# Reciprocal square roots of norms on VectorE: nine two-tensor steps against seven one-tensor steps

## The chip, the cores and the metric

One Trainium2 chip, one of its cores. The time is that of one execution of the whole program on the device, in microseconds (us); a smaller one is better. The program has five engines that matter here: TensorE (PE, with its weight loads PEld), VectorE (DVE), ScalarE (ACT), GpSimd (POOL) and SyncE (SP), which issues the DMAs. Each works through its own queue in order.

## What is computed

Two blocks of a network on one sequence of 1024 tokens with 1024 features, in float32. The first block has a layer A (a gated linear recurrence beside latent attention) and an SSD layer (a chunked state-space scan); the second has a gated feed-forward, a mixing layer (dilated attention beside a diagonal state-space model) and a second feed-forward. What matters here are the norms, one reciprocal root for each token (and, in the SSD layer, for each group of 512 features):

```python
def _rmsnorm(x, g, eps=1e-6):
    y = xf * lax.rsqrt(jnp.mean(xf * xf, axis=-1, keepdims=True) + eps)
def _layernorm(x, g, b, eps=1e-5):
    y = xc * lax.rsqrt(var + eps) * g + b
...
    yg = yg * lax.rsqrt(jnp.mean(yg * yg, axis=-1, keepdims=True) + 1e-6)
...
        x = x + 0.5 * rms_norm(swiglu(h, ...), ffn_post_g)
        h = rms_norm(x, mix_pre_g)
```

## The kernel before

Products run on TensorE in float32r, with every factor split into a high and a low part (`split`, L138 to L141: ScalarE copies the high part, VectorE or GpSimd subtracts). Tokens lie on the 128 partitions in the parts that concern us, in 8 tiles of 128 tokens, so a norm needs one number for each partition: a column of 128x1.

`rsqrt_col` (L264) makes the reciprocal root of such a column on VectorE, with no table of ScalarE. It forms a = v * scale + eps (L270), a first guess from the bits of a taken as an integer (L271), turns a into -a/2 (L272), and makes three Newton rounds of a product c = (y * a) * y (L275) and a step y = (c + 1.5) * y (L280); a factor `mul` other than 1 costs one more instruction (L282). At L275 the operand `a` stands in the place of a scalar read from a column, while `y` is read as two tensors; at L280 `c` and `y` are two tensors and 1.5 is an immediate. Each instruction needs the result of the one before.

Its callers, all with one column but the first:

- `low` in layer A (L485): two calls with 8 columns at once, before the latent projections, at about 82 and 115 us. Here the product is made with two tensor_tensors (L277, L278).
- `layernorm` (L659, called in `layer_a_out` and in `SsdOut.rest`): 16 calls, tile `rl`. VectorE's L667 and ScalarE's L668 follow, then the gain at L669 (VectorE or GpSimd) and the bias at L670 (GpSimd).
- `norm` in the SSD layer (L963): 32 calls, tile `rs`. ScalarE's square (L967) is in front, ScalarE's scaling (L969) behind; `flip` (L971) then transposes on TensorE and evicts on ScalarE (L977).
- `pre_norm` (L1113): 24 calls, tile `rp`, in `SsdOut.rest`, at the end of the first feed-forward and in `mix_out`. ScalarE squares (L1108), VectorE adds the halves (L1110), ScalarE scales (L1118), and TensorE transposes the result.
- `post_norm` (L1121): 24 calls, tile `ro`: 16 at the ends of the two feed-forwards, with `mul` 0.5, and 8 in `mix_out`, with `mul` 1. VectorE sums the tile from PSUM before it (L1428, L1781), scales behind it (L1126, two tensors from SBUF), and GpSimd adds the residual (L1127; VectorE for the last two tiles).

After `SsdOut.rest` and `mix_out` the operands of the next feed-forward are built from the normed tiles (`Ops.build`, L1153, with sums of quarters at L1177 to L1183, some splits of it on GpSimd), and its weights are combined on GpSimd (L1220 to L1223) and split on VectorE.

In the SSD layer, GpSimd makes four products a chunk (L923, L931 to L933) beside VectorE's clamp of 1024 columns (L924).

The order of instructions on each engine isn't the order of the code alone. The program is traced under a context that plans it from modelled durations of the instructions:

```python
    with tile.TileContext(nc, schedule_with_timeline_sim=True) as tc:   # L1947
```

`issue_after`, `deferred` and `behind` add bounds to that plan by hand, for the products and for some loads.

Of the kernel before, what the change touches and what calls it, by code (L numbers as in the profile page):

```python
# [13 lines left out]
I32 = mybir.dt.int32  # L14
AF = mybir.ActivationFunctionType
ALU = mybir.AluOpType
# [247 lines left out]
def rsqrt_col(K, out, v, n, scale, eps, mul=1.0, tag="rs"):  # L264


    V = K.nc.vector
    t = K.small(3 * n, f"{tag}{n}", bufs=2 if n == 1 else 1)
    a, y, c = (t[:, j * n:(j + 1) * n] for j in range(3))
    V.tensor_scalar(a, v, scale, eps, ALU.mult, ALU.add)  # L270
    V.tensor_scalar(y.bitcast(I32), a.bitcast(I32), -0.5, 1597463007.0, ALU.mult, ALU.add)  # L271
    V.tensor_scalar(a, a, -0.5, None, ALU.mult)  # L272
    for step in range(3):
        if n == 1:
            V.scalar_tensor_tensor(c, y, a, y, ALU.mult, ALU.mult)  # L275
        else:
            V.tensor_tensor(c, y, y, ALU.mult)  # L277
            V.tensor_tensor(c, c, a, ALU.mult)  # L278
        last = step == 2
        V.scalar_tensor_tensor(out if last and mul == 1.0 else y, c, 1.5, y, ALU.add, ALU.mult)  # L280
    if mul != 1.0:
        V.tensor_scalar(out, y, mul, None, ALU.mult)  # L282


def sin_tables(K, pos, cos, sin, ang, n):
# [118 lines left out]
def layer_a(K, I, XT, get):  # L404
# [62 lines left out]
    def low(c0, nt, name, scale):  # L467
        raws = []
        rq = K.Q2()
        ssq = K.B()  # L470
        for m in range(nt):
            a = K.A()
            proj_fm(K, a, wload(K, w_in[:, :, c0 + m * P:c0 + (m + 1) * P], NK, P), get)
            raw, sq = rq[:, m, :], K.S()
            nc.scalar.activation(raw, a, AF.Copy)
            nc.scalar.activation(sq, a, AF.Square)
            for i in range(NT):
                nc.tensor.matmul(ssq[:, m * 8 + i:m * 8 + i + 1], sq[:, i * P:(i + 1) * P], K.ones, start=True, stop=True)
            raws.append(raw)
        r = K.small(8, "rst" + name, bufs=1)  # L480
        v = K.small(8, "rsv" + name, bufs=1)
        nc.vector.tensor_copy(v, ssq[:, 0:8])
        for m in range(1, nt):
            nc.vector.tensor_tensor(v, v, ssq[:, m * 8:m * 8 + 8], ALU.add)
        rsqrt_col(K, r, v, 8, scale, 1e-6)  # L485
        outs = [K.Q2(F32R) for _ in range(nt)]
        for h in range(2):
            b = K.B()
            for q in range(4):
                nc.tensor.matmul(b[:, q * P:(q + 1) * P], r[:, 4 * h + q:4 * h + q + 1].to_broadcast([P, P]), K.ident, start=True, stop=True)  # L490
            for m in range(nt):
                rw = raws[m][:, h * 512:h * 512 + 512]
                nc.vector.scalar_tensor_tensor(rw, rw, col(K, name, m), b, ALU.mult, ALU.mult)
                split(K, outs[m][:, 0, h * 512:h * 512 + 512], outs[m][:, 1, h * 512:h * 512 + 512], rw)
        return outs
# [163 lines left out]
def layernorm(K, z, g, b, pool=False):  # L659

    nc = K.nc
    t = K.small(16, "lnt", bufs=3)
    for h in range(2):
        nc.vector.bn_stats(t[:, 6 * h:6 * h + 6], z[:, 512 * h:512 * h + 512])
    nc.vector.bn_aggr(t[:, 12:14], t[:, 0:12].rearrange("p (a b) -> p a b", a=2))
    rsqrt_col(K, t[:, 14:15], t[:, 13:14], 1, 1.0, 1e-5, tag="rl")
    nc.vector.scalar_tensor_tensor(t[:, 15:16], t[:, 12:13], -1.0, t[:, 14:15], ALU.mult, ALU.mult)  # L667
    nc.scalar.activation(z, z, AF.Identity, bias=t[:, 15:16], scale=t[:, 14:15])  # L668
    (nc.gpsimd if pool else nc.vector).tensor_tensor(z, z, g, ALU.mult)  # L669
    nc.gpsimd.tensor_tensor(z, z, b, ALU.add)  # L670
# [111 lines left out]
def ssd_layer(K, I, get, yd, out):  # L782
# [180 lines left out]
    def norm(n):  # L963
        _, _, xdt, sz, y, _ = held[n]
        nc.vector.tensor_tensor(y, y, sz, ALU.mult)
        t = K.small(2, "yss", bufs=3)
        nc.scalar.activation(xdt, y, AF.Square, accum_out=t[:, 0:1])  # L967
        rsqrt_col(K, t[:, 1:2], t[:, 0:1], 1, 1.0 / 512, 1e-6)
        nc.scalar.activation(y, y, AF.Copy, scale=t[:, 1:2])  # L969
# [981 lines left out]
```

## Time and profile before

| | us |
|---|---|
| median of 3 runs | 3380.14 |
| lowest, highest | 3374.5, 3385.84 |
| the profiled execution's own time | 3382.45 |
| its span in the trace | 3380.6 |

The span runs from the first to the last instruction in the trace; the execution's own time has what lies around it too. In the rows below, L275 is line 275 of the kernel, `ro<-ro` a tile written and read (numbers of buffers left out), `128x1` partitions by columns. A wait in square brackets is idle time of the engine in front of an instruction, with what ended it. A duration of VectorE runs from the start of an instruction to its end, and so includes the time that it stands in the engine without progress.

### The profile page before, as it was taken

What the parts mean: (1) busy time and instruction counts of PE and PEld (TensorE: products, weight loads), DVE (VectorE), ACT (ScalarE), POOL (GpSimd) and SP (SyncE); (2) the same over time, 40 slices, a digit from 0 to 9 for tenths busy, and PEclk for the clock granted to TensorE, in tenths of its full rate; (3) what the DMA queues carried; (4) which work ended last, traced back from release to release, by engine and by line L of the source; (5) the groups of instructions that cost most, each with busy time, mean ns of one, the idle gap of its engine ahead of it and who ended that gap; (6) DMA issues with size and microseconds to landing.
All of it is one profiled execution on the core that took longest, in us unless ns stands there. A gap on an engine that the chain in (4) does not pass through costs nothing. (4 is left out here: it accounts for less than half of the span.)

```text
span 3380.6 us, 42313 instructions
## 1 busy us (share of the span) xinstructions
PE 3094.7 (92%) x15560; PEld 2578.1 (76%) x15560; DVE 2295.6 (68%) x3819; ACT 1628.1 (48%) x2947; POOL 774.4 (23%) x487
## 2 busy tenths in 40 slices
PE   8999898999999888878999989899899699999997
PEld 6877877878787776667778877678787588888776
DVE  6537777275848455888785689835676955555998
ACT  5526534354545422465555434542475655554442
POOL 0000011122322211432233345100000423232543
PEclk9999999999999899989999999999999899999999
DMA  3157342244334544323332520435454422224322
GB/s 126 61 191 229 99 144 83 73 83 109 90 103 87 161 147 135 109 83 125 108 125 87 206 86 27 156 125 212 137 154 137 152 75 76 87 81 139 117 81 112
DMA packets 344959, 398.98 MB, mean 118 GB/s; under 512 B 20656, under 2 KB 270640, under 8 KB 344752
## 3 DMA queue, kind: packets, MB, share of 16 engines
q1 hardware_dynamic: 344752, 396.28, 37.8%
q8 instruction: 123, 2.02, 0.2%
q14 instruction: 84, 0.69, 0.1%
HBM read 279.29 MB, written 116.92 MB: 117 GB/s over the span
## 5 line engine op out<-in xcount | busy, mean ns | idle before, releaser
L141 DVE TENSOR_TENSOR wlo<-wst,whi 128x1024 fp32r<-128x1024 f32 (+1 forms) x190 | 230.4, 1216 | 353.6 <-ACT whi L140 344.8
L185 PE MATMUL pa<-x,whi 128*128 128x512 f32 x1568 | 433.9, 398 | 20.6 <-ACT l L343 14.9
L185 PEld LDWEIGHTS pa<-x,whi 128*128 128x128 f32 x1568 | 294.7, 190 | 85.8 <-ACT l L343 15.8
L140 ACT ACTIVATE whi<-wst 128x1024 fp32r<-128x1024 f32 (+1 forms) x190 | 180.1, 949 | 361.2 <-PE pa L185 94.9
L147 ACT ACTIVATE wst<-wst,pk 128x128 f32<-128x128 f32 (+1 forms) x816 | 251.5, 391 | 185.2 <-DMA wst<-in_ffn_w_in_dram 114.8
L185 PE MATMUL pa<-x,wlo 128*128 128x512 f32 x784 | 245.2, 394 | 3.8 <-DVE wlo L141 3.8
L1257 PE MATMUL pb<-x,whi 128*128 128x512 f32 (+1 forms) x736 | 224.5, 381 | 0.0
L1257 PE MATMUL pa<-x,whi 128*128 128x512 f32 (+1 forms) x736 | 220.7, 382 | 0.6 <-DVE p L1271 0.4
L1336 PE MATMUL pa<-wlo,whi 128*128 128x512 f32 x768 | 186.7, 400 | 15.4 <-DVE wlo L141 13.3
L1336 PE MATMUL pb<-wlo,whi 128*128 128x512 f32 x744 | 181.5, 401 | 14.4 <-DVE wlo L141 14.4
L1336 PEld LDWEIGHTS pa<-wlo,whi 128*128 128x128 f32 x768 | 147.6, 193 | 52.0 <-DVE wlo L141 18.2
L1220 POOL TENSOR_TENSOR s<-wst 128x512 f32<-128x512 f32 x44 | 56.9, 1294 | 568.0 <-ACT wst L147 532.3
L1336 PEld LDWEIGHTS pb<-wlo,whi 128*128 128x128 f32 x744 | 142.9, 193 | 48.9 <-DVE wlo L141 19.1
L185 PEld LDWEIGHTS pa<-x,wlo 128*128 128x128 f32 x784 | 148.2, 190 | 38.3 <-DVE wlo L141 6.4
L923 POOL TENSOR_TENSOR s<-s,p 128x1024 f32<-128x1024 f32 x32 | 62.0, 1939 | 499.2 <-DMA s<-d 425.2
L880 PE MATMUL pa<-whi,x 128*128 128x256 f32 x512 | 149.3, 292 | 11.6 <-ACT l L889 8.6
L1257 PEld LDWEIGHTS pa<-x,whi 128*128 128x128 f32 x736 | 136.3, 189 | 28.0 <-ACT p L1260 1.4
L1257 PEld LDWEIGHTS pb<-x,whi 128*128 128x128 f32 x736 | 136.3, 189 | 26.4 <-issue 0.4
L881 PE MATMUL pa<-wlo,x 128*128 128x256 f32 x512 | 145.8, 285 | 0.0
L882 PE MATMUL pa<-whi,x 128*128 128x256 f32 x512 | 145.7, 285 | 0.0
L140 ACT ACTIVATE whi<-s 128x1024 fp32r<-128x1024 f32 x88 | 93.0, 1057 | 107.2 <-POOL s L1221 56.8
L684 PE MATMUL pa<-whi,s 128*128 128x512 f32 x448 | 132.1, 401 | 9.6 <-ACT s L140 4.6
(581 smaller groups left out, 8048.0 us busy)
## 6 DMA issues: line engine op xcount, KB each, us to landing
wst<-in_ffn_w_in_dram SPq DMA_DIRECT2D x88, 512.0 KB, 3.8
d<-l SPq DMA_DIRECT2D x83, 512.0 KB, 3.4
d<-p SPq DMA_DIRECT2D x82, 512.0 KB, 3.5
x<-d SPq DMA_DIRECT2D x128, 256.0 KB, 5.4
p<-d SPq DMA_DIRECT2D x46, 512.0 KB, 4.9
wst<-in_s_w_in_dram SPq DMA_DIRECT2D x40, 512.0 KB, 4.1
s<-d SPq DMA_DIRECT2D x32, 512.0 KB, 9.5
l<-d SPq DMA_DIRECT2D x24, 512.0 KB, 5.8
```

The costliest lines, as they stand in the source:

```text
L140: K.nc.scalar.activation(hi, src, AF.Copy)
L141: (eng or K.nc.vector).tensor_tensor(lo, src, hi.bitcast(F32), ALU.subtract)
L147: K.nc.scalar.activation(st[:, k, :], st[:, k, :], AF.Copy, scale=col(K, gain, k0 + k))
L185: K.nc.tensor.matmul(ps[:, h:h + 512], w, x[:, h:h + 512], start=k == 0 and m == 0, stop=k == n - 1 and m == 2)
L684: K.nc.tensor.matmul(ps[:, h:h + 512], l, r[:, h:h + 512], start=k == 0 and m == 0, stop=k == n - 1 and m == 2)
L880: nc.tensor.matmul(o, xh, wh, start=k == 0, stop=False)
L881: nc.tensor.matmul(o, xh, wl, start=False, stop=False)
L882: nc.tensor.matmul(o, xl, wh, start=False, stop=k == NK - 1)
L923: nc.gpsimd.tensor_tensor(mv, mv, per_head(csT, P), ALU.subtract)
L1220: G(s1, a21, a22, ALU.add)
L1257: nc.tensor.matmul(p, l[:, k, :], r[:, k, :], start=k + m == 0, stop=k == 3 and m == 2)
L1336: nc.tensor.matmul(bank[j], th[:, a + o:a + o + P], tw[:, b:b + 512], start=c + m == 0, stop=c == n - 1 and m == 2)
```

## The change

`rsqrt_col` alone changes. The value and its factor go into one column h = -(v * scale + eps) / (2 mul^2), by one instruction; the guess is taken from the bits of h, with the constant adjusted for its sign, its half and a scaling k. Then come a Newton round (a square c = (y * y) * h and a step y = (c + 1.5 k^(2/3)) * y) and a round of third order (a square and two steps), with constants that spread the error. The factor `mul` costs no instruction of its own. For one column each of these is a `tensor_scalar`: one tensor and two scalars, of which the squares read both from columns, and the steps one from a column and one from the instruction. For 8 columns the steps are scalar_tensor_tensors with an immediate, and the squares two tensor_tensors. A call makes 7 instructions in place of 9 (or of 10 with a factor), and with 8 columns 9 in place of 12.

```diff
--- before.py
+++ after.py
@@ -264,22 +264,33 @@
 def rsqrt_col(K, out, v, n, scale, eps, mul=1.0, tag="rs"):
 
 
+
     V = K.nc.vector
     t = K.small(3 * n, f"{tag}{n}", bufs=2 if n == 1 else 1)
-    a, y, c = (t[:, j * n:(j + 1) * n] for j in range(3))
-    V.tensor_scalar(a, v, scale, eps, ALU.mult, ALU.add)
-    V.tensor_scalar(y.bitcast(I32), a.bitcast(I32), -0.5, 1597463007.0, ALU.mult, ALU.add)
-    V.tensor_scalar(a, a, -0.5, None, ALU.mult)
-    for step in range(3):
-        if n == 1:
-            V.scalar_tensor_tensor(c, y, a, y, ALU.mult, ALU.mult)
-        else:
+    h, y, c = (t[:, j * n:(j + 1) * n] for j in range(3))
+    k = 1.5 ** 0.2
+    f = -0.5 / (mul * mul)
+    V.tensor_scalar(h, v, scale * f, eps * f, ALU.mult, ALU.add)
+
+    magic = 1597463007.0 - 2.0 ** 30 - 2.0 ** 22 + 2.0 ** 23 * math.log2(k) / 3
+    V.tensor_scalar(y.bitcast(I32), h.bitcast(I32), -0.5, magic, ALU.mult, ALU.add)
+
+    if n == 1:
+
+        step = lambda o, i, a, b: V.tensor_scalar(o, i, a, b, ALU.add, ALU.mult)
+        square = lambda: V.tensor_scalar(c, y, y, h, ALU.mult, ALU.mult)
+    else:
+        step = lambda o, i, a, b: V.scalar_tensor_tensor(o, i, a, b, ALU.add, ALU.mult)
+
+        def square():
             V.tensor_tensor(c, y, y, ALU.mult)
-            V.tensor_tensor(c, c, a, ALU.mult)
-        last = step == 2
-        V.scalar_tensor_tensor(out if last and mul == 1.0 else y, c, 1.5, y, ALU.add, ALU.mult)
-    if mul != 1.0:
-        V.tensor_scalar(out, y, mul, None, ALU.mult)
+            V.tensor_tensor(c, c, h, ALU.mult)
+
+    square()
+    step(y, c, 1.5 * k ** (2.0 / 3), y)
+    square()
+    step(h, c, k ** 2 * 5.0 / 3, c)
+    step(out, h, k ** 4 * 1.25, y)
 
 
 def sin_tables(K, pos, cos, sin, ang, n):
```

## Rows read from the trace of the kernel before

**Rows 1.** The page: busy time of each engine over the whole span.
```profile
span 3380.6 us, 42313 instructions
...
PE 3094.7 (92%) x15560; PEld 2578.1 (76%) x15560; DVE 2295.6 (68%) x3819; ACT 1628.1 (48%) x2947; POOL 774.4 (23%) x487
```

**Rows 2.** Stretches: us, busy PE, PEld, DVE, ACT, POOL (counts), granted clock, DMA, GB/s.
```profile
1370.00:1470.00 100.00, 69.99 (x333) 58.19 (x332) 90.28 (x220) 58.44 (x109) 53.60 (x29) 0.86 0.28 90
...
2130.00:2205.00 75.00, 59.12 (x265) 47.44 (x263) 64.18 (x189) 50.24 (x102) 15.18 (x6) 0.92 0.41 140
...
2620.00:2710.00 90.00, 58.40 (x270) 47.41 (x271) 82.95 (x213) 56.88 (x119) 34.60 (x22) 0.80 0.41 143
```

**Rows 3.** Busy time by stretch of L275 alone, then of L280 alone.
```profile
1370.00:1470.00 100.00, 22.27 (x45) 0.86 0.28 90
2130.00:2205.00 75.00, 13.68 (x48) 0.92 0.41 140
2620.00:2710.00 90.00, 20.11 (x48) 0.80 0.41 143
...
sum 1226.00, DVE 103.23; mean DVE 14.75
...
1370.00:1470.00 100.00, 11.81 (x45) 0.86 0.28 90
2130.00:2205.00 75.00, 11.43 (x48) 0.92 0.41 140
2620.00:2710.00 90.00, 11.23 (x48) 0.80 0.41 143
...
sum 1226.00, DVE 77.28; mean DVE 11.04
```

**Rows 4.** Timeline of the end: start us, us, engine, line, what [idle before <-releaser].
```profile
3340.41 2.40 POOL L1127 TENSOR_TENSOR r<-r,p 128x1024 f32<-128x1024 f32 x1 [3.12 <-issue]
...
3340.57 0.15 DVE L272 TENSOR_SCALAR ro<-ro 128x1 f32<-128x1 f32 x1
...
3340.75 2.07 DVE L275 SCALAR_TENSOR_TENSOR ro<-ro 128x1 f32<-128x1 f32 x1
...
3363.26 0.61 PE L684 MATMUL pa<-whi,q 128*128 128x512 f32 x2
...
3369.48 1.21 DVE L1428 TENSOR_TENSOR p<-p,pa 128x1024 f32<-128x1024 f32 x1
...
3371.99 0.15 DVE L270 TENSOR_SCALAR ro<-pon 128x1 f32<-128x1 f32 x1 [0.16 <-ACT s L1108]
...
3372.55 0.22 DVE L275 SCALAR_TENSOR_TENSOR ro<-ro 128x1 f32<-128x1 f32 x1
3372.81 0.16 DVE L280 SCALAR_TENSOR_TENSOR ro<-ro 128x1 f32<-128x1 f32 x1
...
3374.09 1.28 DVE L1126 SCALAR_TENSOR_TENSOR p<-p,pon,r 128x1024 f32<-128x1024 f32 x1
```

**Rows 5.** Line L272: count, ns min/median/max, first and last start.
```profile
L272 DVE TENSOR_SCALAR rp<-rp x24: 136/148/156, 1374.1 to 2698.4; 128x1 f32<-128x1 f32 x24
```

**Rows 6.** Lines L1498, L1500 and L924: count, ns min/median/max, starts.
```profile
L924 DVE TENSOR_SCALAR s<-s x32: 679/1523/1531, 609.0 to 1318.8; 128x1024 f32<-128x1024 f32 x32
...
L1498 DVE TENSOR_SCALAR l<-l,pk x1: 241/241/241, 1520.7 to 1520.7; 128x32 f32<-128x32 f32 x1
...
L1500 DVE TENSOR_SCALAR l<-l x1: 174/174/174, 1522.5 to 1522.5; 128x32 f32<-128x32 f32 x1
```

**Rows 7.** Timeline of a chunk of the SSD layer.
```profile
1223.10 0.53 DVE L275 SCALAR_TENSOR_TENSOR rs<-rs 128x1 f32<-128x1 f32 x1
...
1223.67 0.97 DVE L280 SCALAR_TENSOR_TENSOR rs<-rs 128x1 f32<-128x1 f32 x1
...
1226.88 0.80 PE L927 MATMUL pb<-q 128*128 128x128 f32 x2 [5.29 <-ACT r L977]
```

**Rows 8.** Timeline of layer A's last tiles.
```profile
532.91 2.24 DVE L280 SCALAR_TENSOR_TENSOR lnt<-rl 128x1 f32<-128x1 f32 x1
```

## The prediction

> **What bounds the kernel now.** I read the page first: TensorE is busy for 3094.7 of 3380.6 us and VectorE for 2295.6 [rows 1]. So most of the kernel is bound by TensorE, and a change on VectorE can pay only where TensorE waits. The busy time by stretches, read next, shows where that is [rows 2]. From 1370 to 1470 us (the end of the SSD layer's output, with the start of the first feed-forward) VectorE is busy for 90 of 100 us and TensorE for 70; from 2620 to 2710 us (the same boundary before the second feed-forward) it is 83 of 90 against 58; from 2130 to 2205 us 64 of 75 against 59. There VectorE, which works its queue in order, sets the pace, and every one of these stretches is full of norms.
>
> Then I took the lines of the reciprocal root one by one. The products at L275 and the steps at L280 are busy for 103.23 and 77.28 us in 288 instructions each [rows 3] (96 calls, three rounds; the two wide calls lie outside the windows). Undisturbed, one takes 0.22 and one 0.16 us [rows 4], that is 63.4 and 46.1 us. So 39.8 + 31.2 = 71 us are not arithmetic. The timeline shows what they are: GpSimd starts a tensor_tensor at 3340.41 for 2.40 us, to 3342.81; VectorE's tensor_scalar of one column at 3340.57 runs inside it in 0.15 us, but the first product, a scalar_tensor_tensor, starts at 3340.75 and ends 2.07 us later, at 3342.82, with GpSimd [rows 4]. Two-tensor instructions wait until GpSimd lets go. One-column tensor_scalars do not: L272 takes at most 156 ns in the 24 pre-norms [rows 5].
>
> **The change part by part.** Nothing moves to another queue, and no DMA is added. *The narrow calls (96).* Nine instructions become seven, and in the 16 feed-forward calls with a factor, ten become seven. The six two-tensor instructions of each are gone; all seven have one tensor and two scalars. Starts of neighbours give the price with the gap: three tensor_scalars from 3371.99 to 3372.55, 0.19 each; a product that reads one scalar from a column 0.26 (3372.55 to 3372.81); a whole call of ten 2.10 (3371.99 to 3374.09), hence one of nine 1.91 [rows 4]. Reading a scalar from a column costs a tensor_scalar 241 - 174 = 67 ns [rows 6], so one of those is 0.26 too. Five of the seven read scalars from columns, and the squares read two. No row has two. The ends are 0.26, if both are fetched together, and 0.26 + 0.07; I take 0.26, being nearest to the one-column row, and 2 x 0.19 + 5 x 0.26 = 1.68 a call (1.82 at the other end). Saved: 0.23 a call of nine, 0.42 a call of ten (0.09 and 0.28 at the other end).
>
> *The waits.* Does a one-column tensor_scalar whose scalars lie in columns wait for GpSimd? No row has one under GpSimd. Below, the row with immediates: never. Above, the two-tensor rows: always. In operation and shape it is nearest to the first, and I take that: the 71 us go. What becomes of them differs by stretch.
>
> *The end (3320 to 3381).* TensorE's last product ends at 3363.26 + 0.61 = 3363.87, yet the last tile's sum (L1428) starts at 3369.48: VectorE is 5.6 us late [rows 4], after four waits like the one at 3340.75. The next instructions behind a call there are L1428, which reads PSUM, and the scaling at L1126, due when GpSimd is long done. So at most 5.6 + 0.42 comes back, and at least the last such wait and call, some 2.3. I take 5.
>
> *The SSD layer's chunks (565 to 1370).* In a chunk, a product takes 0.53 and a step 0.97, together 1.1 over the plain 0.22 and 0.16; ScalarE's scaling stands behind the call, its eviction behind that, and TensorE waits 5.29 us for the eviction [rows 7]. Each chunk of this shape gives 1.1 + 0.23. Four lie between 1150 and 1370 us, and a fifth wait there follows a call without the loss: 4 x 1.33 + 0.23 = 5.5, taken as 5. Before, three TensorE waits have the same chain: 4. The other chunks are hidden by projections that TensorE still has queued; without that cover they would give another 20 x 1.3 = 26, which I leave out. Layer A's last tiles show one wait of 2.24 on the way to TensorE [rows 8]: 2.
>
> *The three boundaries.* The waits there are, from rows 3 against 0.22 and 0.16: 12.4 + 4.6 = 17 us (15 calls), 3.1 + 3.8 = 6.9 (16 calls), 9.6 + 3.6 = 13 (16 calls). The shorter calls add 15 x 0.23 = 3.5, 8 x 0.23 + 8 x 0.42 = 5.2, and 3.7. But VectorE's next two-tensor work, the splits at L141 and the scaling at L1126, can now arrive under GpSimd itself. I let half of the waits come back there, as about half of the work behind a call reads PSUM and half two SBUF tensors: 8.5 + 3.5 = 12, 3.5 + 5.2 = 8.7, 6.5 + 3.7 = 10.2. TensorE's granted clock is 0.80 to 0.92 there [rows 2]; what it may gain is not counted. Part of these stretches waits for loads and for ScalarE, so of these 31 I count 22: 9, 5, and 8. The ends are the waits moved on entirely (3, 2, 3) and nothing moved (20, 12, 16).
>
> *The two wide calls (12 instructions to 9).* Three instructions of about 0.2 us each are saved, twice. They lie in the first 130 us under projections; I cost them at nothing, 1.2 us if that cover were gone.
>
> **Sum.** 5 + 5 + 4 + 2 + 9 + 5 + 8 = 38 us. The profiled execution took 3382.45 us, 2.3 above the median of 3380.14; that is less than what a measurement of this kernel can tell, 0.3% or 10 us. 3382.45 - 38 = **3344**. The ends of the terms give 2 + 2 + 0 + 0 + 3 + 2 + 3 = 12, and 6 + 7 + 4 + 2 + 20 + 12 + 16 = 67, so 3315 to 3370.
>
> **The rivals.** *The waits stay.* The five instructions with column scalars wait for GpSimd as the two-tensor ones do. For it: the scalar column is read from SBUF too, and a tensor_scalar does wait when wide: L924, 1024 columns, takes 1523 ns at the median and 679 at least [rows 6]. Against it: L272 [rows 5]. Then only the shorter calls count, in the places above: 12.4 at the boundaries, some 3 elsewhere, and half of it reaching the end: 8 us, **3374**. The Trainium skill, SBUF — State Buffer, "Who interferes with whom", lists `tensor_scalar` among the operations that can take both ports and meet GpSimd, and an instruction with two SBUF inputs as one that always does. Counting a column scalar as an input, that rule gives this rival; counting tensors alone, my forecast. L924 agrees with it, and L272 shows that one column stays outside.
>
> *The waits move.* All of the boundaries' waits reappear at L141 and L1126. For it: these stand behind the calls in program order. Against: L1428, L1177 and their like read PSUM. 5 + 5 + 4 + 2 + half of 12.4: 22 us, **3360**.
>
> *The plan turns.* The program's order is planned from modelled durations (L1947), and new lengths give a new plan. Slower comes about so: at the boundaries the plan puts long two-tensor splits (L141) under GpSimd's tensor_tensors where now a call stood. Each meeting costs up to GpSimd's 2.4 us [rows 4]. Beyond 38 / 2.4 = 16 further meetings on the path it is a loss; 22 give 3344 + 53 = **3397**. Against it: GpSimd's work does not grow, and the three boundaries hold 47 calls, so half of them would have to turn so.
>
> **How the numbers follow.** The forecast 0.62, the waits move 0.15, the waits stay 0.15, the plan turns 0.08. Faster by over 0.3% means under 3370: nearly all of the first, most of the second, a quarter of the third: 0.77. Within 0.3%: 0.16. Slower: 0.07. The range, 3318 to 3372, takes in the first two and part of the third.
>
> **What would show it.** Right: no instruction of the reciprocal root over 0.35 us, its whole busy time near 96 x 1.4 us, the last sum within 1 us of TensorE's end, and less VectorE time in the three boundaries. Wrong: column-scalar instructions that end together with GpSimd's (the waits stay); L141, L667 or L1126 with more time over their plain length than now (they move); a longer wait of TensorE at a boundary with the calls short (the plan turned). A square of 0.29 us would move each call to the upper price.

## The result, and the profile after

The changed kernel took **3326.56 us** (median of 4 runs, 3325.99 to 3326.95), the kernel before 3377.32 us beside it (4 runs, 3374.27 to 3385.84). The ratio is 0.9848, with a 95% interval from 0.9836 to 0.9860: faster by 51 us. The profiled execution of after took 3326.46 us, with a span of 3324.6; against the span before of 3380.6 that is 56.0 us, 5 more than between the medians, since the profiled execution of before lay 5 us above the median of these 4 runs.

The page of after, its span and busy times (beside [rows 1]):

```profile
span 3324.6 us, 42105 instructions
...
PE 3087.2 (93%) x15560; PEld 2575.9 (77%) x15560; DVE 2226.4 (67%) x3605; ACT 1626.6 (49%) x2947; POOL 780.1 (23%) x487
```

VectorE lost 214 instructions and 69 us, TensorE 7.5 us of busy time with as many instructions. So most of the 56 us are waits of TensorE that are gone.

The changed lines of after, by the tile that they write (count, ns min/median/max). L281 is the square with two scalars from columns, L280 the step with one:

```profile
L281 DVE TENSOR_SCALAR rs<-rs x64: 272/273/276, 681.3 to 1326.2; 128x1 f32<-128x1 f32 x64
...
L281 DVE TENSOR_SCALAR ro<-ro x48: 263/272/275, 2097.9 to 3317.1; 128x1 f32<-128x1 f32 x48
```

```profile
L280 DVE TENSOR_SCALAR ro<-ro x48: 198/214/217, 2098.2 to 3317.4; 128x1 f32<-128x1 f32 x48
```

The maxima are the rows to read. Before, single instructions of the root took 2.07 us under GpSimd [rows 4]; now none of the 192 squares is above 0.276 us, and the steps stay at 0.217. GpSimd has not become rarer (487 instructions as before), and 184 of the 480 squares and steps begin while an instruction of GpSimd has at least 0.3 us to go, so the calls do run under it. The timeline of a chunk of the SSD layer in after shows one (it is the chunk of [rows 7]):

```profile
1197.23 0.15 DVE L273 TENSOR_SCALAR rs<-yss 128x1 f32<-128x1 f32 x1 [0.19 <-ACT r L978]
1197.27 1.04 POOL L942 TENSOR_TENSOR r<-q,p 128x512 f32<-128x512 f32 x1 [1.38 <-ACT r L978]
1197.42 0.15 DVE L276 TENSOR_SCALAR rs<-rs 128x1 int32<-128x1 int32 x1
1197.61 0.27 DVE L281 TENSOR_SCALAR rs<-rs 128x1 f32<-128x1 f32 x1
1197.92 0.21 DVE L280 TENSOR_SCALAR rs<-rs 128x1 f32<-128x1 f32 x1
...
1198.27 1.04 POOL L943 TENSOR_TENSOR r<-q,p 128x512 f32<-128x512 f32 x1
1198.48 0.21 DVE L280 TENSOR_SCALAR rs<-rs 128x1 f32<-128x1 f32 x1
1198.73 0.21 DVE L280 TENSOR_SCALAR yss<-rs 128x1 f32<-128x1 f32 x1
1199.04 0.72 ACT L980 ACTIVATE r<-r,yss 128x512 f32<-128x512 f32 x1 [0.90 <-DVE yss L280]
...
1200.29 0.80 PE L938 MATMUL pb<-q 128*128 128x128 f32 x2 [3.54 <-ACT r L988]
```

GpSimd's two products cover the call from its second instruction to its end, and no instruction is longer for it. ScalarE's scaling follows at once, and TensorE waits 3.54 us for the eviction, where it waited 5.29 [rows 7].

*Where the time came from.* To compare stretches, after is cut at the same products of TensorE as before. Stretches of after (columns as in [rows 2]):

```profile
298.20:454.20 156.00, 140.59 (x898) 124.25 (x898) 114.33 (x233) 90.03 (x200) 0.00 (x0) 0.99 0.44 129
...
555.50:1123.00 567.50, 544.82 (x3345) 476.63 (x3344) 346.50 (x500) 286.04 (x355) 145.65 (x105) 0.99 0.40 97
1123.00:1336.80 213.80, 181.80 (x809) 144.13 (x809) 109.22 (x188) 62.43 (x99) 31.99 (x25) 0.92 0.54 162
1336.80:1433.00 96.20, 70.00 (x334) 57.84 (x333) 78.37 (x192) 58.42 (x110) 56.02 (x30) 0.84 0.29 94
...
2091.70:2158.00 66.30, 56.25 (x261) 45.82 (x260) 54.36 (x148) 49.48 (x102) 15.36 (x6) 0.93 0.46 157
2158.00:2580.50 422.50, 400.36 (x2340) 345.50 (x2338) 246.09 (x421) 207.57 (x408) 0.00 (x0) 0.98 0.49 153
2580.50:2658.40 77.90, 54.13 (x269) 43.60 (x269) 73.52 (x180) 55.69 (x117) 40.99 (x22) 0.87 0.47 166
```

Those of before that have no row ahead of the prediction:

```profile
565.00:1150.00 585.00, 550.02 (x3345) 479.24 (x3344) 365.80 (x548) 286.38 (x355) 146.78 (x105) 0.98 0.40 94
1150.00:1370.00 220.00, 181.55 (x810) 143.69 (x809) 115.68 (x207) 61.98 (x99) 34.35 (x26) 0.92 0.51 157
...
2205.00:2620.00 415.00, 394.01 (x2336) 340.37 (x2334) 245.05 (x420) 206.59 (x407) 0.00 (x0) 1.00 0.50 156
```

The numbers of matmuls agree to within four on each line, so the cuts match to about a microsecond. The lengths, before less after:

| stretch of before (us) | what is there | gained (us) | forecast |
|---|---|---|---|
| 0 to 300 | wide calls | 1.8 | 0 |
| 300 to 460 | no call of the root | 4.0 | 0 |
| 460 to 565 | layer A's end | 3.7 | 2 |
| 565 to 1150 | SSD chunks | **17.5** | 4 |
| 1150 to 1370 | SSD chunks | 6.2 | 5 |
| 1370 to 1470 | first boundary | 3.8 | 9 |
| 1470 to 2130 | feed-forward | 1.3 | 0 |
| 2130 to 2205 | second boundary | 8.7 | 5 |
| 2205 to 2620 | mixing layer | -7.5 | 0 |
| 2620 to 2710 | third boundary | 12.1 | 8 |
| 2710 to the end | feed-forward, end | 4.4 | 5 |
| sum | | 56.0 | 38 |

### The profile page after: what moved, and what is told of

Its sections match the earlier page's. It is cut to its first block, busy times and chain, and to the rows that moved or that the text cites. A ratio compares the mean times of both kernels' runs of the same rounds, so it can differ in the third digit from the quotient of the medians.

```text
span 3324.6 us, 42105 instructions
## 1 busy us (share of the span) xinstructions
PE 3087.2 (93%) x15560; PEld 2575.9 (77%) x15560; DVE 2226.4 (67%) x3605; ACT 1626.6 (49%) x2947; POOL 780.1 (23%) x487
## 5 line engine op out<-in xcount | busy, mean ns | idle before, releaser
L141 DVE TENSOR_TENSOR wlo<-wst,whi 128x1024 fp32r<-128x1024 f32 (+1 forms) x190 | 232.3, 1226 | 349.5 <-ACT whi L140 339.0
L185 PE MATMUL pa<-x,whi 128*128 128x512 f32 x1568 | 429.4, 395 | 14.6 <-ACT l L354 10.2
L185 PEld LDWEIGHTS pa<-x,whi 128*128 128x128 f32 x1568 | 292.1, 189 | 78.4 <-ACT l L354 11.4
L185 PE MATMUL pa<-x,wlo 128*128 128x512 f32 x784 | 244.1, 392 | 0.8 <-DVE wlo L141 0.7
L185 PEld LDWEIGHTS pa<-x,wlo 128*128 128x128 f32 x784 | 147.4, 188 | 34.3 <-DVE wlo L141 2.4
L1268 PE MATMUL pa<-x,wlo 128*128 128x512 f32 (+1 forms) x368 | 140.0, 381 | 1.5 <-DVE wlo L141 1.5
```

Source lines behind the costliest of these rows:

```text
L141: (eng or K.nc.vector).tensor_tensor(lo, src, hi.bitcast(F32), ALU.subtract)
L185: K.nc.tensor.matmul(ps[:, h:h + 512], w, x[:, h:h + 512], start=k == 0 and m == 0, stop=k == n - 1 and m == 2)
L1268: nc.tensor.matmul(p, l[:, k, :], r[:, k, :], start=k + m == 0, stop=k == 3 and m == 2)
```

## The experiments

The theory is that the waits for GpSimd went, because one tensor with column scalars doesn't wait; the first rival, that the shorter calls did it.

**1. The form alone.** Three Newton rounds as before, in nine or ten instructions, but each with one tensor and two scalars.

```diff
     for step in range(3):
         if n == 1:
-            V.scalar_tensor_tensor(c, y, a, y, ALU.mult, ALU.mult)
+            V.tensor_scalar(c, y, y, a, ALU.mult, ALU.mult)
...
-        V.scalar_tensor_tensor(out if last and mul == 1.0 else y, c, 1.5, y, ALU.add, ALU.mult)
+        step_to = V.tensor_scalar if n == 1 else V.scalar_tensor_tensor
+        step_to(out if last and mul == 1.0 else y, c, 1.5, y, ALU.add, ALU.mult)
```

> The three Newton rounds of before with nine (or ten) instructions, each with one tensor and two scalars: the form alone. If the waits for GpSimd are the gain: no instruction of the root over 0.3 us, and about 3340 us, since the call itself gets longer than before undisturbed (3 x 0.19 + 3 x 0.31 + 3 x 0.25 = 2.25 us against 1.91) and gives some 10 us of the gain back. If the number of instructions or the shorter chain is the gain: 3377 us or more.

Measured: 3325.33 us, ratio 0.9848 (0.9828 to 0.9869). All of the gain, with as many instructions as before, and none of them waits; of its products, for one tile:

```profile
L275 DVE TENSOR_SCALAR ro<-ro x72: 260/269/276, 2095.3 to 3315.8; 128x1 f32<-128x1 f32 x72
```

The 3340 expected for this theory were 15 us too high, much as the forecast for the whole change was (17).

**2. The number alone.** The change's seven instructions, with two tensors in five of them.

```diff
-        step = lambda o, i, a, b: V.tensor_scalar(o, i, a, b, ALU.add, ALU.mult)
-        square = lambda: V.tensor_scalar(c, y, y, h, ALU.mult, ALU.mult)
+        step = lambda o, i, a, b: V.scalar_tensor_tensor(o, i, a, b, ALU.add, ALU.mult)
+        square = lambda: V.scalar_tensor_tensor(c, y, h, y, ALU.mult, ALU.mult)
```

> The seven instructions of after, but the squares and steps with two tensors: the number alone. If the waits are the gain: the first two-tensor instruction behind GpSimd's still ends with it, over 50 us of waits stay in the root, and the time is about 3360 us (a call of 1.47 us in place of 1.91, some of it on the path). If the number of instructions or the shorter chain is the gain: about 3327 us, as after.

Measured: 3350.87 us, ratio 0.9921 (0.9904 to 0.9939): half of the gain, 9 us under the 3360 that the waits gave and 24 over the 3327 of the rival. Its squares, by tile:

```profile
L281 DVE SCALAR_TENSOR_TENSOR rs<-rs x64: 219/221/985, 690.6 to 1347.5; 128x1 f32<-128x1 f32 x64
...
L281 DVE SCALAR_TENSOR_TENSOR ro<-ro x48: 210/219/2383, 2120.3 to 3344.4; 128x1 f32<-128x1 f32 x48
```

Undisturbed they are shorter than after's (0.22 against 0.27), but their maxima are those of GpSimd's instructions. Taking every instruction of the root over 0.35 us, and 0.2 off each as its plain length, before has 85 of them with 75 us of waiting, this kernel 69 with 58, the changed kernel none. So the number takes part of the waits with it, as there are fewer instructions to be caught, and shortens the chain; how its 24 us divide between these two, and what the new plan adds, no run shows. The two gains don't add up, since the form alone already takes all the waits.

**3 and 4. The SSD layer alone, and all but it.** The new root only in the 32 calls of the SSD layer (tag `rs`, one column), and only in the others; the rest calls the old function, kept as `rsqrt_old`.

```diff
+    if not (tag == "rs" and n == 1):
+        return rsqrt_old(K, out, v, n, scale, eps, mul, tag)
```

> The new root in the 32 calls of the SSD layer's norm alone. The forecast's terms for it were 4 + 5 = 9 us, so 3368 us. If the trace of after is read by stretches (TensorE's products run ahead by 24 us between layer A's end and the first boundary), 3353 us, with TensorE's waits between 550 and 1150 us down from about 32 to about 20 us and a higher granted clock there. If the lead there came from the new plan alone, about 3377 us.

> The new root everywhere but in the 32 calls of the SSD layer's norm, so the three boundaries, layer A's end and the last tiles. If gains add up by place: after + 24, about 3350 us. By the forecast's terms: after + 9, about 3336 us.

Measured: 3350.95 us (ratio 0.9922, 0.9904 to 0.9940) and 3348.83 us (0.9911, 0.9890 to 0.9932). Against 3374.98 of before in the same session that is 24.0 and 26.2 us, and together 50.2: the parts add up, and the SSD layer is half of the whole, not the 9 us of the forecast. The stretches of the kernel with the SSD layer alone, cut at the same products:

```profile
561.80:1126.90 565.10, 544.33 (x3345) 476.73 (x3344) 348.49 (x500) 286.68 (x355) 146.91 (x106) 0.99 0.40 97
1126.90:1340.20 213.30, 178.50 (x810) 140.64 (x809) 109.13 (x191) 61.60 (x99) 31.70 (x24) 0.94 0.55 162
1340.20:1442.80 102.60, 72.34 (x333) 60.08 (x332) 91.50 (x221) 58.55 (x110) 56.33 (x30) 0.85 0.27 88
```

The layer gains 585 - 565.1 = 19.9 and 220 - 213.3 = 6.7; the first boundary, whose calls are the old ones here, takes 2.6 us longer than the 100 of [rows 2].

These two runs also hold the plan still. In experiment 3 TensorE and GpSimd work the same list in the same order as in the kernel before, in experiment 4 as in the changed kernel, and on ScalarE a single pair of instructions is exchanged. So the SSD layer's half is not the plan's doing. In the other half the order does change: some 265 of TensorE's 15560 products stand elsewhere in the changed kernel than before, and what that is worth there was not separated.

**5 and 6. One waiting instruction put back.** The changed kernel with one more instruction in each of the 96 narrow calls, behind the first square. It changes no value. In experiment 5 it reads two tensors, in 6 one:

```diff
     square()
+    if n == 1:
+        V.tensor_tensor(c, c, c, ALU.max)
```

```diff
     square()
+    if n == 1:
+        V.tensor_scalar(c, c, 1.0, None, ALU.mult)
```

> The changed kernel, with one more instruction in each narrow call, which reads two tensors and changes no value (the larger of c and c, behind the first square). If the gain came from instructions that no longer wait for GpSimd, one waiting instruction in each call brings part of the waits back: some 30 of these 96 instructions take over 0.35 us, together 25 to 35 us over their plain length, and the time goes to 3337 to 3352 us. If the gain came from the shorter calls, one instruction of about 0.2 us gives back a third of it at the very most where calls are on the path: 3327 to 3333 us, and the same as the next kernel.

> The changed kernel, with one more instruction in each narrow call that reads one tensor and changes no value (c times 1.0, behind the first square): the control of the kernel before this one, with as many instructions in the same places. By the waits no added instruction takes over 0.25 us, and the time is 3325 to 3332 us, 10 us or more below the kernel with the two-tensor instruction. By the number of instructions the two take the same time.

Measured: 3349.24 us (3346.28 to 3356.32; ratio 0.9919, 0.9901 to 0.9938) and 3332.38 us (3331.54 to 3336.57; ratio 0.9869, 0.9854 to 0.9884). In both programs every engine works the same list of instructions in the same order, and only the form of the 96 differs, so this pair is the cleanest of the study. The added line with two tensors, for two of its four tiles (busy us, mean ns of one | idle before it):

```profile
L291 DVE TENSOR_TENSOR ro<-ro 128x1 f32<-128x1 f32 x24 | 13.0, 542 | 0.3
L291 DVE TENSOR_TENSOR rs<-rs 128x1 f32<-128x1 f32 x32 | 10.7, 333 | 1.1
```

and with one:

```profile
L291 DVE TENSOR_SCALAR rs<-rs 128x1 f32<-128x1 f32 x32 | 4.9, 154 | 1.1
L291 DVE TENSOR_SCALAR ro<-ro 128x1 f32<-128x1 f32 x24 | 3.6, 150 | 0.3
```

With the tiles `rp` and `rl` (9.5 and 7.3 against 3.5 and 2.4 us) that is 40.5 against 14.4 us: 26.1 us of waiting, in one instruction of eight. The kernel is 3349.24 - 3332.38 = 16.9 us longer, so two thirds of such a wait reach the end. The control lies at the upper end of what was expected, and 3332.38 - 3327.31 = 5.1 us above experiment 8, for 14.4 us of added work, 18 with the gaps. That would be three tenths of what only lengthens a call, but it is a rough price: single executions of the two overlap (3331.54 to 3336.57 against 3324.55 to 3332.57), and some 166 of TensorE's products stand in another order. As expected of the waits, 30 of the 96 take over 0.35 us. The longest, in the timeline of experiment 5:

```profile
2136.60 2.40 POOL L1140 TENSOR_TENSOR l<-l,p 128x1024 f32<-128x1024 f32 x1 [4.72 <-DVE p L1139]
2136.68 2.33 DVE L291 TENSOR_TENSOR rp<-rp 128x1 f32<-128x1 f32 x1
```

GpSimd ends at 2139.00 and VectorE at 2139.01.

**7. The remaining narrow two-tensor instructions.** In the changed kernel, the layer norm's product (L678) and the sum of squares (L1121) as one tensor and a column scalar.

```diff
-    nc.vector.scalar_tensor_tensor(t[:, 15:16], t[:, 12:13], -1.0, t[:, 14:15], ALU.mult, ALU.mult)
+    nc.vector.tensor_scalar(t[:, 15:16], t[:, 12:13], -1.0, t[:, 14:15], ALU.mult, ALU.mult)
...
-        K.nc.vector.tensor_tensor(t[:, 0:1], t[:, 0:1], t[:, 1:2], ALU.add)
+        K.nc.vector.tensor_scalar(t[:, 0:1], t[:, 0:1], t[:, 1:2], None, ALU.add)
```

> The changed kernel, with the two other one-column two-tensor instructions that remain, in the layer norm and in the sum of squares, written as one tensor and a column scalar as well. By the waits, the 13 us that these two stand behind GpSimd go, at the same places, and a fourth to two thirds of it reaches the end: 3317 to 3324 us. If what is left of the waits only moves to the next wide instruction, 3325 to 3328 us.

Measured: **3321.62 us** (3320.29 to 3323.57), ratio 0.9834 (0.9817 to 0.9851): below the changed kernel's runs of the same session (3324.55 to 3332.57) with no overlap, by 5.7 us between the medians. It is the fastest kernel of the study. The plan moved a little here too (some 48 of TensorE's products), and its part is not separated. L1121 in after, for one of its two tiles:

```profile
L1121 DVE TENSOR_TENSOR pon<-pon x8: 147/632/2372, 2583.4 to 2626.9; 128x1 f32<-128x1 f32 x8
```

and here:

```profile
L1121 DVE TENSOR_SCALAR pon<-pon x8: 199/204/215, 2583.0 to 2624.0; 128x1 f32<-128x1 f32 x8
```

Each of these is 50 ns longer undisturbed, and the waits of up to 2.37 us are gone.

**8. The changed kernel again**, beside experiments 5 to 7.

> The changed kernel once more, beside the three others on the same chip: 3325 to 3328 us, so that differences of 3 us or more between the others and it can be told.

Measured: 3327.31 us (3324.55 to 3332.57), ratio 0.9853 (0.9837 to 0.9870). The median is where it was; single executions spread by 8 us here.

## Why the prediction was right, and where not

The time came out 17 us below the forecast of 3344 and inside its range, near the lower end, and the case is the one forecast: the waits are gone. Of the 17, 5 us lie in the starting value (3382.45, where the four runs beside the change have a median of 3377.32) and 13 in the gain, 51 us instead of 38. (The text gives its range as 3315 to 3370 from the terms and as 3318 to 3372 at its end; the time lies in both.) By its steps:

- **What a call costs: right.** Forecast 1.68, at the other end 1.82. In the chunk above, starts follow each other by 0.19 (the first two), 0.31 (squares) and 0.25 (steps): 2 x 0.19 + 2 x 0.31 + 3 x 0.25 = 1.75, halfway. Reading a second scalar from a column costs 273 - 214 = 59 ns, much like the first, so the lower end, both fetched together, is not what was measured. The whole busy time of the 96 calls is 141 us, 1.47 each, where the text asked for about 1.4.
- **The column scalars don't wait: right.** No row of before showed it; the maxima of 0.217 and 0.276 us do. The rival "the waits stay" falls with them. By the Trainium skill, SBUF — State Buffer, "Who interferes with whom", an instruction with two SBUF inputs meets a GpSimd instruction that reads SBUF (the prediction's "always" leaves out this condition; GpSimd's products, sums and splits here all read SBUF). By these maxima, only tensors count as inputs there, and scalars from columns don't.
- **The SSD layer: 9 forecast, 23.7 measured.** This is the term that was mis-sized. The step that failed is "The other chunks are hidden by projections that TensorE still has queued", with only three of TensorE's waits counted before 1150 us. The timeline of a chunk of before shows the chain, at one of what look to be those three (at 732, 892 and 1056 us, the longest of this kind):

```profile
727.43 0.97 DVE L280 SCALAR_TENSOR_TENSOR rs<-rs 128x1 f32<-128x1 f32 x1
...
729.39 0.72 ACT L969 ACTIVATE p<-p,yss 128x512 f32<-128x512 f32 x1 [1.24 <-DVE yss L280]
730.02 1.00 ACT L342 ACTIVATE raw<-pa 128x1024 f32<-128x1024 f32 x1
...
730.92 1.20 ACT L343 ACTIVATE l<-pa,pk 128x1024 f32<-128x1024 f32 x1
...
732.17 1.22 PE L185 MATMUL pa<-x,whi 128*128 128x512 f32 x2 [4.27 <-ACT l L343]
```

  ScalarE waits 1.24 us for the root, and behind the scaling stand, in its queue, the two instructions that read the finished projection out of PSUM; the next projection (L185) can start only after them. So the late root holds up TensorE by way of another chain than its own. The same place in after:

```profile
716.43 0.72 ACT L980 ACTIVATE p<-p,yss 128x512 f32<-128x512 f32 x1
...
719.21 0.96 PE L185 MATMUL pa<-x,whi 128*128 128x512 f32 x3 [2.49 <-ACT l L354]
```

  ScalarE no longer waits, and TensorE 1.78 us less. The three waits went from 13.5 to 7.7 us together: 5.8, where 4 were forecast. TensorE's waits by what ended them show how many more places there are; of before, from 565 to 1150 us (us in total, times, longest):

```profile
PE pa L185 <- ACT l L343: 14.9, 4, 5.3
PE pa L880 <- ACT l L889: 8.6, 4, 4.0
PE pa L185 <- ACT l L889: 4.1, 2, 3.2
PE pa L185 <- DVE wlo L141: 3.3, 4, 1.5
```

  and of after in the same stretch:

```profile
PE pa L185 <- ACT l L354: 10.2, 5, 3.9
PE pa L891 <- ACT l L900: 7.6, 4, 3.7
PE pa L185 <- ACT l L900: 2.2, 1, 2.2
...
PE pa L185 <- DVE wlo L141: 0.2, 1, 0.2
```

  With a smaller group each (3.0 us in 3 waits before, 1.3 in 1 after), 33.9 us in 17 waits became 21.5 in 12: 12.4 us. So 6.6 us came from waits that the prediction counted at nothing. About half of them are in the last line: TensorE waits for the low part of the next projection's weights, which VectorE itself splits (L141), and three of these four splits stood in VectorE's queue right behind a call. A projection that is still queued is therefore no cover when its weights wait for the same late engine. The other 5.2 are TensorE's busy time, 544.82 instead of 550.02 us for the same 3345 instructions, at a granted clock of 0.99 instead of 0.98. In the other profiles this busy time is 4.7 to 5.7 us below that of before in experiments 3, 6, 7 and 8, and 1.5 us at most in 2, 4 and 5, where waits remain in the SSD layer; but experiment 1, without waits, has only 2.8, so this part is less firmly the change's. With the 26 us that the text named for a missing cover the stretch would have had 30; the 17.5 lie halfway, so part of the cover held.
- **The boundaries: 22 forecast, 24.6 measured** (3.8, 8.7 and 12.1 for 9, 5 and 8). That the sum came so near is partly luck, as the single terms miss by 4 to 5 us either way. VectorE's busy time there fell from 237.4 [rows 2] to 206.3 us. Half of the waits were to return at the next wide instructions. Counting for all of VectorE's instructions what each takes over its plain length (where that is over a quarter of a microsecond), 24.1 us of waits became 13.5 at the first boundary, though the root itself lost 17: 7 came back, chiefly at the splits, as these lines of after show (their maxima before were 2.21 and 1.48 us):

```profile
L141 DVE TENSOR_TENSOR s<-s x5: 677/909/2616, 1337.0 to 1375.9; 128x512 fp32r<-128x512 f32 x5
L141 DVE TENSOR_TENSOR l<-l x4: 412/677/2571, 1342.9 to 1368.9; 128x256 fp32r<-128x256 f32 x4
```

  At the second, 10.5 us became 2.9, so next to nothing came back. At the third, 21 became 12, though the root itself lost 15: 6 came back, at the splits and at L1121 (its line in after stands in experiment 7). So two fifths came back at two places of three, a little less than the half assumed, and the rival "the waits move", which lets all of them come back, holds at none. Why the first boundary gained least, with the most waits gone, no run shows.
- **The end: 5 forecast, 5 measured.** Before, TensorE's last product ended at 3363.87, 16.7 us ahead of the end of the span; now it ends at 3312.53 + 0.61 = 3313.14, 11.5 us ahead, and the last tile's sum starts 0.5 us behind it, as the forecast asked for (columns as in [rows 4]):

```profile
3312.53 0.61 PE L695 MATMUL pa<-whi,q 128*128 128x512 f32 x2
3313.68 1.21 DVE L1439 TENSOR_TENSOR p<-p,pa 128x1024 f32<-128x1024 f32 x1
```

  The stretch's 4.4 us in the table are these 5.2, less 0.8 given back ahead of them.
- **Layer A: 2 forecast, 3.7 measured. The wide calls: nothing forecast;** the 1.8 us of the first 300 us are no sign of them, since the repeat of the same kernel shows none (its products there stand 0.8 us later than before's).
- **The granted clock, "not counted": it went both ways.** From 300 to 460 us no narrow call has run yet, and 4.0 us were gained, by TensorE at its higher clock (below). From 2205 to 2620 us 7.5 us were given back, of which 400.36 - 394.01 = 6.4 are TensorE's busy time (with four products more), at a granted clock of 0.98 instead of 1.00; no instruction of the root runs in it. Both sizes vary between profiled executions: in the first stretch experiment 2 gained nothing; in the second the repeat of the same kernel gave back as much, and experiment 4, with the same order of products, 0.9.
- **The plan turned** did not happen: 24.6 us fewer at the three boundaries.

What is not settled: what three instructions fewer are worth once the waits are gone. Experiment 1 (nine or ten instructions) took as long as the change (seven), while experiment 6 puts one instruction a call at 5 us, with the overlap said there. The planned order of TensorE's products differs between experiment 1 and the change too, and by its stretches it gained 7.7 us more than the change from 1150 to 1372 us and lost about as much at the boundaries and the end; the two effects were not separated.

## What to carry to other kernels

Where VectorE and GpSimd work at the same time, look at the maxima of VectorE's smallest instructions, not at their means: a 128x1 step of 0.16 us that shows 2 us stands behind GpSimd, and the chain that waits for it paid two thirds of that here (16.9 of 26.1 us). A step on one column that reads its second operand as a scalar from a column, instead of as a second tensor, costs some 55 ns more undisturbed and doesn't stand there; here this was worth more than fewer instructions (49.7 us in experiment 1 against 24.1 in experiment 2). When pricing what a late engine costs, list everything that TensorE waits for in the stretch, instead of following one chain and assuming that queued work hides the rest.

## What the runs showed of the hardware

A scalar from a column costs 60 ns each on a 128x1 tensor_scalar: 0.15 us with none (L273), 0.214 with one, 0.273 with two. The two-tensor form with one column scalar and two tensors took 0.22 undisturbed, so it is the cheaper one where GpSimd is idle.

How long a two-tensor instruction stands is exact. Of the 96 of experiment 5, each either ran beside no instruction of GpSimd and took 0.14 to 0.16 us, or began while GpSimd was working and ended 14 to 21 ns after GpSimd's instruction did. In the SSD layer the median is only 0.32 us because GpSimd's product is nearly done there when the chain arrives.

TensorE's clock moved time where nothing was changed. From 330 to 350 us, before:

```profile
330.00:350.00 20.00, 18.22 (x98) 16.16 (x96) 11.34 (x27) 9.80 (x24) 0.00 (x0) 0.83 0.49 136
```

and the same work in after:

```profile
328.20:344.80 16.60, 15.48 (x99) 13.66 (x98) 11.27 (x27) 9.91 (x24) 0.00 (x0) 1.00 0.57 162
```

Part of the 20 us was at the lower level of 1.2 GHz, and 3.4 us went with it. The kernel of experiment 3, which is the kernel before up to the SSD layer, gained 3.5 us in the stretch from 300 to 460 us as well. So some 4 of the 56 us between the two profiles belong to the execution that was profiled and not to the change.
